# Splitting the key, value and query weights during the input projections, and starting the context attention inside the Fourier projection

## The chip, the cores and the metric

One core of one Trainium2 chip runs the whole program. The metric is the device time of that core in microseconds (us).

## What is computed

Two layers of a hybrid mixer over 512 latent tokens (stream X) and 256 context tokens (stream C), model width 1024, in float32. Cut to what matters here:

```python
for l in range(DEPTH):
    mod = silu_c @ w_mod[l] + b_mod[l]            # six rows: shift, scale, gate, twice
    h = x * (1 + sc1) + sh1
    proj = h @ w_in[l]                            # columns: A query/key-value/rope, B spatial gate, D pooling, C Fourier
    cq, ckv = rms_norm(proj[q]) , rms_norm(proj[kv])
    q = cq @ w_uq[l];  k = ckv @ w_uk[l];  v = ckv @ w_uv[l]
    attn = softmax(q k^T) v                       # 8 heads; context attends to context only
    mix = concat(attn, spatial_gating(proj), multiscale_pool(proj), fourier_mix(proj))
    x = layer_norm(ALPHA * x + g1 * (mix @ w_out[l]))
    x = layer_norm(ALPHA * x + g2 * swiglu(x * (1 + sc2) + sh2))
```

In layer 0 all four groups are computed for both streams, in layer 1 for X alone, with the context's keys and values.

## The kernel before

Every float32 product is made of three products of rounded halves. `split` (L167 to L169) turns a tile into a high part (a cast on ScalarE, L168) and a low part (a subtraction on VectorE, L169), and `mm3` (L172 to L174) issues low by high, high by low, high by high on TensorE.

A weight tile of the input projection is loaded by SyncE into a staging buffer (pool `S4`, four buffers, `wload`, L186) and split into a buffer of pool `W8` (five buffers). The projection's column groups have two weight tiles each, one per half of the 1024 rows: D0 and D4 for pooling, C0 and C4 for Fourier. `mods` (L268 to L308) computes later modulation rows from 512 KB tiles of `w_mod`, which go through the same `S4` buffers; L282 is their product, L301 and L308 their way into `modT`. Their steps are handed out by `fill` between the products of `chunk_d` and `chunk_c`, so that the loads of the next modulation run beside the projection.

After the A group, each layer calls `chunk_b` (gate columns, with a layer norm of 256 columns on VectorE and GpSimd, L375 to L541), `chunk_d` (pooling columns, four outputs in layer 0, two in layer 1, each of 24 products), `pool_sums` (running sums, L841 to L861), `spatial` (transposes at L811, products, gate at L822, transposes at L827), `pool_proj`, then `phase("att")`, which closes the scratch pool of the projections ("inp", ten buffers from `I`) and opens the attention's. Then come `make_ckv` (transposes at L602 and L606), `qkv_weights`, in layer 1 `make_cq` of X, and `chunk_c` (Fourier columns). `qkv_weights` loads `w_uk` and `w_uv` (L613, L614) into one `S4` tile and scales it (L615) and splits it, and loads the two halves of `w_uq` (L622), each into an `S4` tile, scales them (L625), splits them and copies rope columns on GpSimd (L632).

In layer 0 `chunk_c` runs to its end for both streams; then follow `make_cq(C)`, the Fourier transform and the context attention, which makes a head's query one step ahead of its scores (`make_q` for head h + 1 beside `scores` of head h).

The program is written in this order, but a scheduler that simulates the engines sets the final, fixed order of instructions on each engine, and with it which buffer of a pool each tile gets. Engines run their lists in that order. What it sets around the change is shown with the change, below.

Of the kernel before, what the change touches and what calls it, by code (L numbers as in the profile page):

```python
# [90 lines left out]
def hybrid_kernel(ctx: ExitStack, tc: tile.TileContext, out: bass.AP, g: dict):  # L91
# [453 lines left out]
    def chunk_c(l, streams):  # L545

        ws = [getw(("C", l, 0), 0), getw(("C", l, 4), 0)]
        for st in streams[::-1]:
# [16 lines left out]
            v = lambda ap: ap.rearrange("p n c -> p (n c)")  # L565
            split(v(st.f[0]), v(st.f[1]), pd[:, :n])

    def chunk_d(l, streams):
# [42 lines left out]
    def qkv_weights(l):  # L611
        st4 = S4(D)
        nc.sync.dma_start(out=st4[:, 0:512], in_=g["w_uk"][l])  # L613
# [6 lines left out]
        for k in range(2):  # L620
            st4 = S4(768)
            nc.sync.dma_start(out=st4, in_=g["w_uq"][l][k * P:(k + 1) * P, :])  # L622
            sc = ST(1)
            G_.tensor_scalar(out=sc, in0=pv(l, PQ, k), scalar1=QSCALE, scalar2=None, op0=ALU.mult)
            V_.tensor_scalar(out=st4, in0=st4, scalar1=sc, scalar2=None, op0=ALU.mult)  # L625
            w = W8()
            sv = st4.rearrange("p (h c) -> p h c", h=NH)
            wv = [w[:, i, :D].rearrange("p (h c) -> p h c", h=NH) for i in range(2)]
            split(wv[0][:, :, 0:96], wv[1][:, :, 0:96], sv)
            for i in range(2):  # L630
                for d_, s_ in ((96, 72), (104, 64), (112, 88), (120, 80)):
                    G_.tensor_copy(wv[i][:, :, d_:d_ + 8], wv[i][:, :, s_:s_ + 8])  # L632
            wq.append(wv)
# [118 lines left out]
    def attention(st, vt, wkv, wq):  # L752
# [30 lines left out]
        make_k(0, wkv, st)  # L783
        q[0] = make_q(st, 0, wq)
        for i, (h, qp) in enumerate(steps):
            if h % 2 == 0 and qp == 0:
                rv[h // 2] = rvp.tile([P, NTX, 2], F32, tag="rv", name=nm("rv"))
            es[(h, qp)] = scores(st, h, qp, q[h], rv[h // 2])
            if qp == 0 and h % 2 and h < NH - 1:
                make_k(h // 2 + 1, wkv, st)  # L790
            if qp == 0 and h < NH - 1:
                q[h + 1] = make_q(st, h + 1, wq)
            j = i - lagt
# [636 lines left out]
    for l in range(2):  # L1430
# [9 lines left out]
        if l == 1:  # L1440
            phase("inp")
        chunk_b(l, act)
        pts = chunk_d(l, act)
        dds = pool_sums(l, act, pts)
# [9 lines left out]
        if l == 1:  # L1454
            make_ckv(X, at)
        wkv, wq = qkv_weights(l)
        if l == 1:
            make_cq(X, at)
        chunk_c(l, act)
        fill(99)  # L1460
        if l == 0:
            make_cq(C, at)
        vt = []
        fo = fourier(l, act)
        if l == 0:
            values(wkv, vt, range(NTC))
            ac = attention(C, vt, wkv, wq)
            for i in range(NH):
# [57 lines left out]
```

## Time and profile before

| what | value |
|---|---|
| median of three runs | 1662.52 us (1662.23 to 1663.35) |
| profiled execution | 1662.84 us |
| its span | 1661.1 us |
| mean granted TensorE clock | 0.984 of full speed |
| TensorE busy | 1571.1 us, 95% |
| VectorE busy | 1048.2 us, 63% |
| ScalarE busy | 770.5 us, 46% |

The span is the stretch from the first to the last instruction that the profiler recorded; what lies around it is 1.7 us. The chain of work that ended last lies on TensorE for 80% of the span, on VectorE for 7%, on DMA for 5% and on ScalarE for 4%. The changed code runs at about 100 to 225 us (layer 0) and 1060 to 1120 us (layer 1).

### The profile page before, as it was taken

The numbers are of one execution on the slowest core, as the hardware profiler recorded it, in microseconds if no ns is written. First come the engines' busy times: TensorE is split into PE (matmuls) and PEld (weight loads), VectorE is DVE, ScalarE is ACT, GpSimd is POOL, SyncE is SP. The second block draws the span as 40 slices with busy tenths as digits, with TensorE's granted clock in tenths as the row PEclk, the third lists the DMA queues.
The fourth block names the chain that finished last, engine by engine and source line by source line (L and its number), as shares of the span: only waits on it lengthen the run. The fifth ranks groups of instructions, "written<-read, shape, count | busy, mean of one in ns | idle before, by whom it ended". The sixth has DMA issues, their size and how long they took to land.

```text
span 1661.1 us, 23839 instructions
## 1 busy us (share of the span) xinstructions
PE 1571.1 (95%) x9129; PEld 1357.4 (82%) x9129; DVE 1048.2 (63%) x1591; ACT 770.5 (46%) x1371; POOL 259.5 (16%) x322
## 2 busy tenths in 40 slices
PE   6999889999999999999999798989999999998897
PEld 3756778897899999997666486779988999997686
DVE  1433686876775656655435438577857888886835
ACT  2521675874643434434223525467954655554220
POOL 0213011430000000001205005243311000001302
PEclk9999999999999999999999898999999999999999
DMA  9566114118422323439886725411146344457321
GB/s 322 185 217 204 39 39 140 39 58 296 126 83 83 105 93 105 130 124 326 300 289 212 234 79 186 135 58 39 39 145 202 104 128 127 128 184 265 115 89 51
DMA packets 180502, 241.80 MB, mean 146 GB/s; under 512 B 10874, under 2 KB 127468, under 8 KB 180388
## 3 DMA queue, kind: packets, MB, share of 16 engines
q1 hardware_dynamic: 180388, 240.28, 44.7%
q8 instruction: 72, 1.18, 0.3%
q14 instruction: 42, 0.34, 0.1%
HBM read 215.30 MB, written 24.94 MB: 145 GB/s over the span
## 4 chain that ended last, share of the span: by engine, by line
PE 80%; DVE 7%; DMA 5%; ACT 4%; issue 2%; SPq 0%; POOL 0%; POOLq 0%; DVEq 0%; ACTq 0%
PE pd L1197 22%; PE pd L172 10%; PE pd L173 9%; PE pd L174 9%; PE ps L172 6%; PE ps L173 5%; PE ps L174 5%; PE ps L1197 4%; PE ps L282 3%; PE ps L739 3%; PE ps L723 2%; DVE w L169 2%; DVE u L169 2%; DMA s<-in_w_in_dram 2%; ACT w L168 1%
## 5 line engine op out<-in xcount | busy, mean ns | idle before, releaser
L169 DVE TENSOR_TENSOR w<-s,w 128x1024 fp32r<-128x1024 f32 (+3 forms) x285 | 353.9, 1248 | 276.5 <-ACT w L168 275.9
L168 ACT CAST w<-s 128x1024 fp32r<-128x1024 f32 (+3 forms) x285 | 292.8, 1030 | 464.7 <-PE pd L174 113.2
L1197 PE MATMUL pd<-u,w 128*128 128x256 f32 (+1 forms) x1938 | 298.3, 307 | 10.0 <-DVE w L169 8.7
L1197 PEld LDWEIGHTS pd<-u,w 128*128 128x128 f32 x1938 | 281.3, 190 | 16.6 <-DVE w L169 10.0
L172 PE MATMUL pd<-w,u 128*128 128x512 f32 (+5 forms) x728 | 276.8, 382 | 10.1 <-DVE u L169 3.1
L173 PE MATMUL pd<-w,u 128*128 128x512 f32 (+5 forms) x728 | 273.5, 376 | 1.7 <-DVE w L169 1.7
L174 PE MATMUL pd<-w,u 128*128 128x512 f32 (+5 forms) x728 | 271.0, 373 | 0.0
L172 PEld LDWEIGHTS pd<-w,u 128*128 128x128 f32 x728 | 139.4, 192 | 60.2 <-issue 19.3
L173 PEld LDWEIGHTS pd<-w,u 128*128 128x128 f32 x728 | 139.4, 192 | 29.1 <-issue 5.0
L174 PEld LDWEIGHTS pd<-w,u 128*128 128x128 f32 x728 | 139.3, 191 | 26.2 <-issue 3.4
L168 ACT CAST u<-y 128x512 fp32r<-128x512 f32 (+2 forms) x178 | 94.0, 546 | 76.8 <-DMA y<-yd 45.2
L169 DVE TENSOR_TENSOR u<-y,u 128x512 fp32r<-128x512 f32 (+2 forms) x118 | 79.4, 695 | 58.7 <-ACT u L168 52.6
L169 POOL TENSOR_TENSOR u<-y,u 128x512 fp32r<-128x512 f32 (+1 forms) x60 | 79.5, 1331 | 229.1 <-ACT u L168 207.5
L172 PE MATMUL ps<-u,w 128*128 128x256 f32 (+2 forms) x288 | 91.8, 327 | 1.8 <-DVE modT L308 1.2
L173 PE MATMUL ps<-u,w 128*128 128x256 f32 (+2 forms) x288 | 93.5, 327 | 0.1
L174 PE MATMUL ps<-u,w 128*128 128x256 f32 (+2 forms) x288 | 93.5, 327 | 0.0
L172 PE MATMUL ps<-w,u 128*128 128x512 f32 (+1 forms) x208 | 81.2, 399 | 6.1 <-DVE u L169 5.2
L173 PE MATMUL ps<-w,u 128*128 128x512 f32 (+1 forms) x208 | 82.2, 396 | 3.0 <-DVE w L169 3.0
L169 DVE TENSOR_TENSOR u<-ps,u 128x512 fp32r<-128x512 f32 (+2 forms) x106 | 66.9, 655 | 28.1 <-ACT u L168 27.0
L174 PE MATMUL ps<-w,u 128*128 128x512 f32 (+1 forms) x208 | 81.4, 392 | 0.0
L1313 POOL TENSOR_TENSOR f<-f,f 128x1024 f32<-128x1024 f32 x10 | 24.2, 2434 | 327.1 <-DMA f<-rd 248.5
L1197 PE MATMUL ps<-u,w 128*128 128x384 f32 (+1 forms) x456 | 73.8, 311 | 0.0
(250 smaller groups left out, 2588.8 us busy)
## 6 DMA issues: line engine op xcount, KB each, us to landing
s<-in_w_ffn_dram SPq DMA_DIRECT2D x154, 512.0 KB
s<-in_w_out_dram SPq DMA_DIRECT2D x50, 512.0 KB
u<-in_w_mod_dram SPq DMA_DIRECT2D x48, 512.0 KB
s<-in_w_mod_dram SPq DMA_DIRECT2D x48, 512.0 KB
s<-in_w_in_dram SPq DMA_DIRECT2D x16, 512.0 KB
yd<-f SPq DMA_DIRECT2D x19, 384.0 KB
y<-yd SPq DMA_DIRECT2D x88, 64.0 KB
y<-yd SPq DMA_DIRECT2D x22, 256.0 KB
```

Source lines behind the costliest of these rows:

```text
L168: A_.copy(out=hi, in_=src)
L169: (eng or V_).tensor_tensor(out=lo, in0=src, in1=f(hi), op=ALU.subtract)
L172: T_.matmul(ps, lhsT=ll, rhs=rh, start=start, stop=False)
L173: T_.matmul(ps, lhsT=lh, rhs=rl, start=False, stop=False)
L174: T_.matmul(ps, lhsT=lh, rhs=rh, start=False, stop=stop)
L282: T_.matmul(ps[32 * j:32 * j + 32, :n], lhsT=sst[:, k, :], rhs=ws[j // 2][:, (j % 2) * n:(j % 2 + 1) * n], start=(k == 0), stop=(k == KD - ...
L723: T_.transpose(pt[:, o:o + P], es[t2][:, k * P:(k + 1) * P], ident)
L739: T_.matmul(av[:, 0:256], lhsT=vt[k][:, h, :], rhs=pts[k // 2][:, a, (k % 2) * 256:(k % 2 + 1) * 256], start=(k == 0 and a == 1), stop=(k ...
L1197: T_.matmul(ps, lhsT=A[u][:, k], rhs=B[k][:, v], start=first and k == 0 and i == 0, stop=last and k == 3 and i == 2, skip_group_check=True)
L1313: G_.tensor_tensor(out=y, in0=y, in1=bc[0], op=ALU.mult)
```

## The change

`qkv_weights` is called right after `chunk_b`, ahead of `chunk_d`, and its staging tiles come from the scratch pool `I` in place of `S4`. `chunk_c` becomes a generator that stops after each stream, the context stream first. In layer 0, after that stop, `make_cq(C)` runs and the context attention starts: `make_k` for the first head pair and `make_q` for heads 0 and 1. Then `chunk_c` goes on with X. The context attention from there on makes its queries two heads ahead. No arithmetic is added or removed. In the listing of the changed kernel lines after L567 stand 1 later, after L785 6 later.

```diff
--- before.py
+++ after.py
@@ -564,6 +564,7 @@
                         w[0][:, k % 4], w[1][:, k % 4], k == 0, k == KD - 1)
             v = lambda ap: ap.rearrange("p n c -> p (n c)")
             split(v(st.f[0]), v(st.f[1]), pd[:, :n])
+            yield
 
     def chunk_d(l, streams):
 
@@ -609,7 +610,7 @@
             G_.tensor_copy(kT[i][64:P, :, sl], kT[0][64:P, :, sl])
 
     def qkv_weights(l):
-        st4 = S4(D)
+        st4 = I(n=D)
         nc.sync.dma_start(out=st4[:, 0:512], in_=g["w_uk"][l])
         nc.sync.dma_start(out=st4[:, 512:], in_=g["w_uv"][l])
         V_.tensor_scalar(out=st4, in0=st4, scalar1=pv(l, PKV, 0), scalar2=None, op0=ALU.mult)
@@ -618,7 +619,7 @@
 
         wq = []
         for k in range(2):
-            st4 = S4(768)
+            st4 = I(n=768)
             nc.sync.dma_start(out=st4, in_=g["w_uq"][l][k * P:(k + 1) * P, :])
             sc = ST(1)
             G_.tensor_scalar(out=sc, in0=pv(l, PQ, k), scalar1=QSCALE, scalar2=None, op0=ALU.mult)
@@ -782,14 +783,19 @@
 
         make_k(0, wkv, st)
         q[0] = make_q(st, 0, wq)
+        qa = 1
+        if st.s:
+            q[1] = make_q(st, 1, wq)
+            qa = 2
+            yield
         for i, (h, qp) in enumerate(steps):
             if h % 2 == 0 and qp == 0:
                 rv[h // 2] = rvp.tile([P, NTX, 2], F32, tag="rv", name=nm("rv"))
             es[(h, qp)] = scores(st, h, qp, q[h], rv[h // 2])
             if qp == 0 and h % 2 and h < NH - 1:
                 make_k(h // 2 + 1, wkv, st)
-            if qp == 0 and h < NH - 1:
-                q[h + 1] = make_q(st, h + 1, wq)
+            if qp == 0 and h < NH - qa:
+                q[h + qa] = make_q(st, h + qa, wq)
             j = i - lagt
             if j >= 0:
                 pts[steps[j]] = turn(st, es.pop(steps[j]))
@@ -1440,6 +1446,7 @@
         if l == 1:
             phase("inp")
         chunk_b(l, act)
+        wkv, wq = qkv_weights(l)
         pts = chunk_d(l, act)
         dds = pool_sums(l, act, pts)
         ahead(index[("C", l, 4)] + 1)
@@ -1453,18 +1460,20 @@
         make_ckv(C, at)
         if l == 1:
             make_ckv(X, at)
-        wkv, wq = qkv_weights(l)
+        vt = []
         if l == 1:
             make_cq(X, at)
-        chunk_c(l, act)
+        cc = chunk_c(l, act)
+        if l == 0:
+            next(cc)
+            make_cq(C, at)
+            ac = attention(C, vt, wkv, wq)
+            next(ac)
+        run(cc)
         fill(99)
-        if l == 0:
-            make_cq(C, at)
-        vt = []
         fo = fourier(l, act)
         if l == 0:
             values(wkv, vt, range(NTC))
-            ac = attention(C, vt, wkv, wq)
             for i in range(NH):
                 next(ac)
                 if i == XPREP:
```

The scheduler gives the instructions another order. In the order rows below `s`, `w` and `i` are buffers of `S4`, `W8` and `I`, the last number names the tile.

First place: SyncE in layer 0, from the loads of D4, C0 and C4 (L186) on. Before:

```order
L186 DMA s_159_1040<-in_w_in_dram 128x4x256
L186 DMA s_161_1045<-in_w_in_dram 128x4x256
L186 DMA s_163_1050<-in_w_in_dram 128x4x256
L268 DMA s_169_1074<-in_w_mod_dram 128x1024
L294 DMA gd<-y_1057 2x512 x2
L245 DMA y_1068<-in_b_mod_dram 2x512 x4
L268 DMA s_170_1076<-in_w_mod_dram 128x1024
L268 DMA s_172_1083<-in_w_mod_dram 128x1024
L268 DMA s_173_1085<-in_w_mod_dram 128x1024
L268 DMA s_175_1117<-in_w_mod_dram 128x1024
L874 DMA y_1367<-in_w_pool_dram 64x64 x4
```

And now:

```order
L186 DMA s_167_1079<-in_w_in_dram 128x4x256
L186 DMA s_169_1084<-in_w_in_dram 128x4x256
L186 DMA s_171_1089<-in_w_in_dram 128x4x256
L268 DMA s_177_1113<-in_w_mod_dram 128x1024
L294 DMA gd<-y_1096 2x512 x2
L245 DMA y_1107<-in_b_mod_dram 2x512 x4
L880 DMA y_1406<-in_w_pool_dram 64x64
L268 DMA s_178_1115<-in_w_mod_dram 128x1024
L880 DMA y_1406<-in_w_pool_dram 64x64 x3
L268 DMA s_180_1122<-in_w_mod_dram 128x1024
L614 DMA i_1040<-in_w_uk_dram 128x512
L615 DMA i_1040<-in_w_uv_dram 128x512
```

The four loads of `w_uk`, `w_uv` and `w_uq` (L614, L615, L623) now stand between the third and the fourth load of `w_mod` instead of behind all of them and `w_spatial`.

Second place: VectorE in layer 0. Tile 1040 before is D4, 1045 is C0, 1050 is C4. Before, from the split of D0 on:

```order
L169 TENSOR_TENSOR w_134_908<-s_133_907,w_134_908 128x1024
L169 TENSOR_TENSOR w_160_1041<-s_159_1040,w_160_1041 128x1024
L288 TENSOR_TENSOR y_1057<-ps_744,y_734 128x512
L169 TENSOR_TENSOR w_162_1046<-s_161_1045,w_162_1046 128x1024
L382 BN_STATS bn_971<-pd_730 128x6
L384 BN_AGGR st_973<-bn_971 128x2
L538 SCALAR_TENSOR_TENSOR i_968<-pd_730,st_973,y_964 128x256
L541 SCALAR_TENSOR_TENSOR i_968<-i_968,st_973,y_964 128x256
L169 TENSOR_TENSOR w_164_1051<-s_163_1050,w_164_1051 128x1024
```

Now D4 is tile 1079, and its split is the last of these rows, 39 rows behind D0's:

```order
L169 TENSOR_TENSOR i_1017<-i_1016,i_1017 128x256 x2
L616 TENSOR_SCALAR i_1040<-i_1040,PV 128x1024
L626 TENSOR_SCALAR i_1047<-i_1047,st_1049 128x768
L169 TENSOR_TENSOR w_160_1044<-i_1040,w_160_1044 128x1024
L626 TENSOR_SCALAR i_1063<-i_1063,st_1065 128x768
L169 TENSOR_TENSOR w_163_1052<-i_1047,w_163_1052 128x8x96
L169 TENSOR_TENSOR w_166_1068<-i_1063,w_166_1068 128x8x96
L169 TENSOR_TENSOR w_168_1080<-s_167_1079,w_168_1080 128x1024
```

The splits of D4, C0 and C4 left the place right behind D0's split; D4's now follows the scaling and splitting of the query, key and value weights, and C0's (tile 1085) and C4's (1090) come further behind, with pooling sums between.

TensorE in layer 0, where the first product with D4 stands (`w_168_1080` is D4 split, tiles 1122 and 1124 are loads of `w_mod`):

```order
L173 MATMUL ps_1216<-u_424,w_134_908 128x512
L174 MATMUL ps_1216<-u_424,w_134_908 128x512
L282 MATMUL ps_1117<-s_180_1122,sst 32x512 x2
L282 MATMUL ps_1117<-s_181_1124,sst 32x512 x2
L172 MATMUL ps_1130<-u_481,w_168_1080 128x512
L173 MATMUL ps_1130<-u_481,w_168_1080 128x512
```

Before, the 24 products of a pooling output (12 with D0, 12 with D4) stood in one row behind the first L282; now the twelve with D4 come after 36 with D0 and after four L282 rows, two of which follow each other. Of the 144 Fourier products (L172 to L174 with C0 and C4), 108 stood behind the transposes of `spatial` (L811) before; 52 stand behind them (L817) now, 56 went ahead of them.

Third place: TensorE in layer 1. Before, all 48 pooling products came first, then the transposes of `spatial` and the Fourier products:

```order
L173 MATMUL ps_9411<-u_8777,w_1479_9367 128x512
L174 MATMUL ps_9411<-u_8777,w_1479_9367 128x512
L811 MATMUL ps_9469<-ident,s_1496_9467 128x128 x4
L172 MATMUL pd_9631<-w_1481_9372,u_8721 128x256
L173 MATMUL pd_9631<-w_1481_9372,u_8721 128x256
L174 MATMUL pd_9631<-w_1481_9372,u_8721 128x256
```

Now the transposes (L817) come after 24 products with D0, and behind them one product with C0 (`w_1489_9411`) and then those with D4 (`w_1487_9406`):

```order
L174 MATMUL ps_9450<-u_8745,w_1464_9287 128x512
L817 MATMUL ps_9508<-ident,s_1504_9506 128x128 x4
L172 MATMUL pd_9631<-w_1489_9411,u_8721 128x256
L172 MATMUL ps_9516<-i_9320,u_9513 128x256
L172 MATMUL ps_9521<-i_9320,u_9513 128x256
L172 MATMUL ps_9422<-u_8753,w_1487_9406 128x512
L173 MATMUL ps_9422<-u_8753,w_1487_9406 128x512
```

VectorE in layer 1, ahead of these (9406 is D4, 9411 is C0 in their split forms; 9370, 9378 and 9394 are the key and value and the query weights):

```order
L626 TENSOR_SCALAR i_9373<-i_9373,st_9375 128x768
L538 SCALAR_TENSOR_TENSOR i_9319<-pd_9176,st_9357,y_9315 128x256
L626 TENSOR_SCALAR i_9389<-i_9389,st_9391 128x768
L169 TENSOR_TENSOR w_1479_9370<-i_9366,w_1479_9370 128x1024
L541 SCALAR_TENSOR_TENSOR i_9319<-i_9319,st_9357,y_9315 128x256
L169 TENSOR_TENSOR u_9513<-ps_9508,u_9513 128x512
L169 TENSOR_TENSOR w_1482_9378<-i_9373,w_1482_9378 128x8x96
L169 TENSOR_TENSOR w_1485_9394<-i_9389,w_1485_9394 128x8x96
L169 TENSOR_TENSOR w_1487_9406<-s_1486_9405,w_1487_9406 128x1024
L169 TENSOR_TENSOR w_1489_9411<-s_1488_9410,w_1489_9411 128x1024
```

D4 and C0 are split behind the three query, key and value splits; before, D4 was split ahead of the layer norm's rows (L382 to L541). On ScalarE the casts stand in the same succession, C0's as the last.

## Rows read from the trace of the kernel before

**Rows 1.** The profile page: span, TensorE's busy time, the chain by engine.

```profile
span 1661.1 us, 23839 instructions
...
PE 1571.1 (95%) x9129; PEld 1357.4 (82%) x9129; DVE 1048.2 (63%) x1591; ACT 770.5 (46%) x1371; POOL 259.5 (16%) x322
...
PE 80%; DVE 7%; DMA 5%; ACT 4%; issue 2%; SPq 0%; POOL 0%; POOLq 0%; DVEq 0%; ACTq 0%
```

**Rows 2.** Busy time by window, layer 0; columns: window, length, engines, PEclk, DMA, GB/s.

```profile
150.00:160.00 10.00, 10.00 (x75) 8.19 (x74) 5.82 (x6) 3.10 (x4) 5.72 (x7) 1.00 0.76 232
...
170.00:180.00 10.00, 6.72 (x42) 4.99 (x42) 8.82 (x23) 8.80 (x18) 0.00 (x0) 1.00 0.33 106
```

**Rows 3.** The same windows, layer 1.

```profile
1070.00:1080.00 10.00, 10.00 (x45) 8.09 (x44) 9.15 (x23) 4.89 (x10) 6.26 (x13) 1.00 0.32 94
```

**Rows 4.** Timeline of TensorE, layer 0: start us, us, instruction, idle before it.

```profile
112.74 1.05 PE L282 MATMUL ps<-s,sst 128*32 128x512 f32 x4
115.01 0.47 PE L172 MATMUL ps<-u,w 128*128 128x512 f32 x1 [1.22 <-DVE modT L308]
```

**Rows 5.** Chain of waits, layer 0, two loads of 512 KB: start us, us, what.

```profile
101.29 3.75 DMA s<-in_w_in_dram
...
107.44 3.90 DMA s<-in_w_in_dram
```

**Rows 6.** Timeline of TensorE, layer 1.

```profile
1069.85 0.39 PE L172 MATMUL ps<-u,w 128*128 128x512 f32 x1
...
1081.01 0.60 PE L811 MATMUL ps<-ident,s 128*128 128x128 f32 x4
...
1082.15 0.28 PE L172 MATMUL pd<-w,u 128*128 128x256 f32 x1
...
1084.51 0.28 PE L174 MATMUL pd<-w,u 128*128 128x256 f32 x1
...
1098.36 0.63 PE L606 MATMUL ps<-ident,u 128*128 128x128 f32 x4 [0.87 <-ACT y L884]
```

**Rows 7.** Timeline of SyncE's queue, layer 0.

```profile
148.73 0.33 SPq L613 DMA_DIRECT2D s<-in_w_uk_dram  x1
```

**Rows 8.** Timeline of VectorE, layer 0.

```profile
153.68 0.75 DVE L615 TENSOR_SCALAR s<-s,PV 128x1024 f32<-128x1024 f32 x1 [14.45 <-DMA s<-in_w_uv_dram]
```

**Rows 9.** Timeline of VectorE, layer 1.

```profile
1061.85 1.23 DVE L169 TENSOR_TENSOR w<-s,w 128x1024 fp32r<-128x1024 f32 x1
...
1075.60 0.42 DVE L382 BATCH_NORM_STATS2 bn<-pd 128x6 f32<-128x256 f32 x1
1075.94 0.41 DVE L169 TENSOR_TENSOR i<-i,i 128x256 fp32r<-128x256 f32 x1
...
1076.95 0.61 DVE L625 TENSOR_SCALAR s<-s,st 128x768 f32<-128x768 f32 x1
1077.48 0.48 DVE L538 SCALAR_TENSOR_TENSOR i<-pd,st,y 128x256 f32<-128x256 f32 x1
...
1080.34 0.94 DVE L169 TENSOR_TENSOR w<-s,w 128x768 fp32r<-128x768 f32 x1
...
1083.52 0.68 DVE L169 TENSOR_TENSOR u<-ps,u 128x512 fp32r<-128x512 f32 x1
```

**Rows 10.** Shorter windows of layer 0.

```profile
192.00:194.00 2.00, 0.97 (x9) 0.83 (x8) 1.17 (x4) 1.43 (x7) 0.00 (x0) 1.00 0.00 0
194.00:196.00 2.00, 1.41 (x11) 1.44 (x12) 1.85 (x4) 0.84 (x2) 0.00 (x0) 0.96 0.00 0
196.00:198.00 2.00, 2.00 (x12) 2.00 (x11) 0.97 (x3) 1.49 (x7) 0.00 (x0) 0.50 0.00 0
```

**Rows 11.** Timeline of ScalarE, layer 1.

```profile
1070.05 1.05 ACT L168 CAST w<-s 128x1024 fp32r<-128x1024 f32 x1 [2.21 <-PE pd L174]
...
1078.41 0.84 ACT L168 CAST w<-s 128x768 fp32r<-128x768 f32 x1
```

## The prediction, made before the run

> **What bounds the kernel now.** I read the page first: of a span of 1661.1 us TensorE is busy for 95%, and the chain that ended last lies on it for 80% [rows 1]. So a change that adds and removes no arithmetic is worth what it does to TensorE's idle time and to its granted clock. The windows of the two changed stretches come next, and they differ. While the query, key and value weights are scaled and split in layer 0, TensorE is busy for 10.00 of 10 us in the window from 150; it idles from 170 on, 3.28 of 10 us, in the attention's start [rows 2]. In layer 1 it is busy for 10.00 of 10 where pooling is projected [rows 3]. The splits that the change moves are therefore covered where they stand now; what they can be worth elsewhere is the idle time behind 170, and what they can cost lies where they go.
>
> The timelines and the chain then give durations. The L282 products on one `w_mod` load took 1.05 us [rows 4]. A 512 KB load took 3.75 and 3.90 us [rows 5]. A product of 512 columns takes a slot of 0.233 us: 48 of them lie between 1069.85 and 1081.01. One of 256 columns takes 0.118 us: 20 slots lie between 1082.15 and 1084.51 [rows 6].
>
> **Layer 0: the staging buffers.** The loads of D4, C0 and C4 are still issued right behind D0's, but their splits now stand behind the query, key and value splits, and the buffers bear it out: `W8` has five, handed out to D0, the three weights and D4 in this order, and C0 and C4 take D0's and D4's when these come free. So three of the four `S4` buffers hold unsplit tiles, and the loads of `w_mod` take turns in the one that is left: each is issued when the L282 of the load before it has ended, and lands 3.75 us later. I walk TensorE's new list from the point where both kernels agree, the first L282 of this modulation, which ends at 113.8 [rows 4].
> - Before, the next product waited 1.22 us for L308, which stood behind the last of the three splits on VectorE [rows 4]. That split is gone from there: -1.2.
> - Twelve products with D0 take 2.8 us, to 116.6. The second load was issued at 113.8 and lands at 117.5: +0.9. Its L282 ends at 118.5.
> - Twelve products of 256 and twelve of 512 columns take 1.4 and 2.8, to 122.7. The third load, issued at 118.5, is there. Its L282 ends at 123.7.
> - The next row is the L282 of the fourth load, issued at 123.7 at the earliest: it lands at 127.5. +3.8. It ends at 128.5.
> - The next product needs the low part of D4. The weights' four loads stand in SyncE's list behind the third `w_mod` load; before, 4.95 us passed from the issue of `w_uk` at 148.73 to the scaling at 153.68 [rows 7, 8]. Issued at 118.9, they let VectorE begin at 123.9. In front of D4's end lie one scaling of 0.75 [rows 8], two of 0.61, splits of 1.23, 0.94 and 0.94, and D4's own 1.23 [rows 9], 6.3 with what I round, so 130.3: +1.8.
>
> Sum for this stretch: +5.3. The bounds of the waits on loads: nothing, if the buffers come free earlier than the order says, and 8 us, if the loads lie beside the weights' 1.3 MB and take twice as long.
>
> **Layer 0: the attention's start.** Here the change does what it says: the context's queries and keys start in the middle of the Fourier products, and the next query stands two heads ahead. What could go is the idle time of 170 to 180, 3.28 us [rows 2], the idle 1.03 and 0.59 us between 192 and 196, and the stretch at a granted clock of 0.50 behind them, which from 194 to 202 costs 3.1 us [rows 10] (the row at 196 stands for three windows alike): 8.0 together. Against that, 56 of the 108 Fourier products that stood behind the transposes of `spatial` are ahead of them now. They are 56 x 0.118 = 6.6 us of work that covered the chains of `spatial` and pooling. I take 8.0 - 6.6 = 1.4 as the gain; the ends are 0 and 8.0. It is nearer the low end because each of these chains goes transposes, cast, subtraction, product, gate, and has no other work between.
>
> **Layer 1: the second place.** Before, D4 was split at 1061.85 [rows 9], ahead of the layer norm, and TensorE ran 48 pooling products without a pause [rows 6]. Now only 24 with D0 stand in front; they and the transposes are through at 1069.85 + 24 x 0.233 + 0.4 = 1075.9. The next row needs the high part of C0, which is the last cast of a row on ScalarE: the second weight tile's scaling, then casts of 0.84, 1.05 and 1.05 [rows 11]. VectorE reached the third tile's statistics at 1075.60 [rows 9], with the key and value split (1.23) already behind it. Without that split in front I set this at 1075.0. Up to the end of the last scaling follow 0.42, 0.41, 0.75, 0.61, 0.48, 0.61 and two short pieces, 0.6 together, so 1078.9 [rows 8, 9]; the casts end at 1081.8. TensorE waits 5.9 us. Then D4's low part: from 1078.9 VectorE has 1.23, 0.48, 0.68, 0.94, 0.94 and D4's 1.23 to do [rows 9], to 1084.4. Three products lie between, so the second wait is 1.8. Together +7.7, with bounds of 5 (ScalarE and VectorE close up the gaps between their rows) and 9. Fifteen Fourier products are left over behind this, and they cover the wait of 0.87 before the rope transposes at 1098.36 [rows 6]: -0.9. Net +6.8.
>
> **The clock.** Pauses of 1.03 and 0.59 us were followed by a granted clock of 0.50 [rows 10], the lower of the two levels, 1.2 GHz; but 3.28 idle us in ten left it at 1.00 [rows 2]. The new pauses, 3.8 and 1.8 us with one us of work between, and 5.9 and 1.8 with three products between, are longer than either. I take one fall in each layer at the 3.1 us of that row: +6.2. A slower TensorE gives the other engines the same time to catch up, and the short waits behind both places, about one us in each layer, go under it: -2.0. Without both falls this term is 0, with a third one +7.3. The Trainium skill, in "TensorE: Matmul & The Clock Gate", section "HAM oscillation — how this bites in real kernels", says that a wait for data that is long enough halves the clock of the products behind it, and advises to put the products of one tile together before one waits for the next; this speaks against the new order, in which D0's and D4's products are taken apart. By that rule both falls come, and the sum stands as it is; by the 170 window alone it would be 4.2 less.
>
> **Costed at nothing:** the rope copies and the two scalings of `sc` on GpSimd, which are moved ahead of its pooling sums and are through before TensorE hands over the pooling columns that these sum; the two more query buffers, since `U` has 22; the reordering behind the common point in both layers, where the lists agree again.
>
> **The sum.** 5.3 - 1.4 + 6.8 + 6.2 - 2.0 = +14.9 on the profiled execution's 1662.84 us: 1677.7. The median of the runs is 0.3 lower, so 1677.4.
>
> **Rivals.**
> 1. The waits come, the clock stays. For it: the window at 170 [rows 2]. Against it: the pauses are three times as long as those that were followed by a fall. +10.7: 1673.2. With one fall, 1675.3. Chance 0.3 together.
> 2. Faster: the change does what it says, and no wait takes the place. Then -1.2 at 115, the whole 8.0 behind 170 at best, -0.9 in layer 1; with half of the 8.0, -6: 1656.5. The point that decides is whether D4's split in layer 0 is done when its first product comes up, which asks that the weights land by 118 and not 124; the 4.95 us from issue to use [rows 7, 8] speak against it. The Trainium skill, "DMA: Bandwidth & Descriptors", section "Rules for kernel authors", speaks for it: issue a transfer early, compute, wait late. By that rule moving the weights' loads ahead by 30 us is a gain. The trace shows VectorE idle for 14.45 us before the scaling [rows 8] while TensorE is busy for 10.00 of 10 [rows 2], so the time so gained is not TensorE's. Chance 0.11.
> 3. Even: the reordered attention gives back its 8.0, the clock holds, and layer 1's wait is at its low end. 4.1 + 5 - 8 = about +1, so 1663.5. Chance 0.05 for within 0.2%, and as much for a little above it.
> 4. Worse: loads that take twice as long beside each other, and a third fall, +6 more: 1683. Chance 0.09.
>
> **The numbers.** My forecast has 0.4. 0.2%, 3.3 us, is about what a measurement of this kernel can tell from no change. The range from 1662 to 1684 takes in the forecast, rivals 1, 3 and 4, and leaves out 2 and what lies beyond. Faster 0.11, same 0.05, slower 0.84.
>
> **What would show it.** In layer 0, around 123 to 131, two waits of TensorE, one on a `w_mod` load before an L282, one on VectorE before the first product with D4; loads of `w_mod` one after the other through one buffer; the granted clock at 0.5 for some us behind. In layer 1, a wait of about 6 us on ScalarE's cast behind the transposes of `spatial`, then a shorter one on D4's subtraction, where the window from 1070 had none. Around 170 to 200, fewer idle us than before. Wrong would be: pooling's products without a pause in either layer, D4 split ahead of the query weights, or a total that comes from another stretch.

## The result, and the profile after

The changed kernel is slower by about 1%: 1680.9 us (median of 4, 1680.06 to 1681.76) against 1662.93 us (median of 4), a ratio of 1.0103 with a 95% interval of 1.0088 to 1.0119. The forecast was 1677.4 us, the range 1662 to 1684. Measured again later (e10), beside 20 runs of the kernel before, the ratio was 1.0116 (1.0094 to 1.0138).

The page of the profiled execution (1680.06 us); it answers to [rows 1]:

```profile
span 1678.3 us, 23832 instructions
...
PE 1577.6 (94%) x9129; PEld 1360.9 (81%) x9129; DVE 1044.9 (62%) x1591; ACT 770.1 (46%) x1371; POOL 265.0 (16%) x322
...
PE 80%; DVE 9%; DMA 5%; ACT 4%; issue 2%; POOL 0%; SPq 0%; DVEq 0%; POOLq 0%; ACTq 0%
```

TensorE's busy time grew by 6.5 us although it issues the same 9129 products, and the span by 17.2. What is added is idle time and products at the lower clock, in places that the windows name. First four of layer 0, then one of layer 1; they answer to [rows 2, 3] (the columns are those of [rows 2]):

```profile
120.00:130.00 10.00, 5.96 (x32) 3.73 (x28) 5.25 (x11) 4.02 (x9) 2.41 (x5) 0.99 0.71 236
130.00:140.00 10.00, 8.69 (x31) 4.82 (x33) 3.12 (x4) 2.37 (x3) 5.06 (x15) 0.67 0.37 112
...
170.00:180.00 10.00, 9.20 (x78) 8.82 (x76) 4.78 (x8) 3.63 (x5) 0.00 (x0) 1.00 0.24 71
180.00:190.00 10.00, 6.84 (x40) 5.08 (x40) 7.62 (x22) 6.68 (x17) 0.00 (x0) 1.00 0.30 101
...
1080.00:1090.00 10.00, 4.45 (x15) 3.30 (x14) 9.22 (x14) 5.46 (x8) 9.19 (x20) 0.77 0.33 79
```

In layer 0 the window from 120 has only 5.96 busy us of 10, and the one from 130 a granted clock of 0.67. In layer 1, which now begins about 5 us later, the window from 1080 has 4.45 of 10 where [rows 3] had 10.00 from 1070. TensorE's timeline names the waits (in brackets the idle time and what ended it): five of layer 0, three of layer 1, one at the end of the program.

```profile
114.38 1.05 PE L282 MATMUL ps<-s,sst 128*32 128x512 f32 x4 [0.75 <-DMA s<-in_w_mod_dram]
...
119.47 1.05 PE L282 MATMUL ps<-s,sst 128*32 128x512 f32 x4 [1.07 <-DMA s<-in_w_mod_dram]
121.06 0.39 PE L172 MATMUL ps<-u,w 128*128 128x256 f32 x1 [0.53 <-ACT i L540]
...
130.12 1.92 PE L282 MATMUL ps<-s,sst 128*32 128x512 f32 x4 [3.63 <-DMA s<-in_w_mod_dram]
133.23 0.79 PE L172 MATMUL ps<-u,w 128*128 128x512 f32 x1 [1.19 <-DVE w L169]
...
1086.00 0.58 PE L172 MATMUL pd<-w,u 128*128 128x256 f32 x1 [4.92 <-ACT w L168]
...
1087.73 0.80 PE L172 MATMUL ps<-u,w 128*128 128x512 f32 x1 [0.63 <-DVE w L169]
...
1116.12 0.75 PE L172 MATMUL ps<-w,ckvT 128*128 128x512 f32 x1 [2.91 <-DVE kT L169]
...
1570.87 0.80 PE L173 MATMUL ps<-w,u 128*128 128x512 f32 x1 [6.94 <-DVE w L169]
```

Shorter windows show what follows the pauses: the clock falls to 0.50, the 1.2 GHz level, four times in the changed stretches. It does so behind 130, behind 1086 and behind 1116, and from 191 to 194 behind five short waits of the attention's start (0.87, 0.36, 0.21, 0.42 and 0.57 us between 185 and 190.2).

```profile
128.00:130.00 2.00, 0.00 (x0) 0.00 (x0) 2.00 (x4) 0.83 (x1) 0.72 (x2) 0.94 0.60 224
130.00:132.00 2.00, 1.88 (x4) 0.19 (x4) 1.95 (x4) 1.78 (x2) 2.00 (x4) 0.50 0.00 0
132.00:134.00 2.00, 0.81 (x4) 0.67 (x3) 1.18 (x1) 0.00 (x0) 2.00 (x7) 0.50 0.44 76
134.00:136.00 2.00, 2.00 (x7) 1.52 (x6) 0.00 (x0) 0.00 (x0) 1.06 (x6) 0.50 0.94 369
136.00:138.00 2.00, 2.00 (x9) 1.28 (x9) 0.00 (x0) 0.11 (x1) 0.00 (x0) 0.86 0.24 88
...
190.00:192.00 2.00, 1.87 (x10) 1.70 (x11) 1.69 (x5) 0.26 (x1) 1.17 (x2) 0.80 0.00 0
192.00:194.00 2.00, 2.00 (x8) 1.71 (x7) 1.27 (x3) 1.78 (x5) 0.00 (x0) 0.50 0.00 0
...
1084.00:1086.00 2.00, 0.00 (x1) 0.01 (x1) 2.00 (x4) 2.00 (x4) 2.00 (x6) 0.87 0.18 67
1086.00:1088.00 2.00, 1.37 (x4) 1.05 (x5) 2.00 (x3) 0.25 (x1) 2.00 (x3) 0.50 0.00 0
...
1116.00:1118.00 2.00, 1.88 (x5) 1.49 (x6) 1.97 (x4) 1.06 (x3) 1.87 (x2) 0.55 0.73 199
1118.00:1120.00 2.00, 2.00 (x7) 1.59 (x6) 2.00 (x4) 0.94 (x2) 0.16 (x1) 0.60 0.35 141
```

A place that both kernels pass tells how much was lost by then. Taken from the two timelines of TensorE:

| place | before | after | difference | gained or lost there | forecast |
|---|---|---|---|---|---|
| bias transposes (L231), unchanged code | 65.84 | 66.86 | +1.0 | +1.0 | 0 |
| transposes of `spatial`, layer 0 (less 6.6 us of products moved ahead of them) | 153.80 | 169.66 | +9.3 | +8.3 | 5.3 + 3.1 |
| nine softmax transposes of the context attention (L723, L724) | 246.42 | 252.55 | +6.1 | -3.2 | -1.4 - 1.0 |
| last transposes of layer 1's projection (L368), same order | 1040.11 | 1045.22 | +5.1 | -1.0 | 0 |
| last softmax transposes, layer 1 | 1220.80 | 1235.48 | +14.7 | +9.6 | 6.8 + 3.1 - 1.0 |
| end of the span | 1661.1 | 1678.3 | +17.2 | +2.5 | 0 |

The two forecast places carry 8.3 and 9.6 us. In the first row and the fourth the lists of TensorE are the same in both kernels; that they cancel out is chance. The last row was not forecast.

Three more views show the mechanism. SyncE's queue in layer 0: the second, third and fourth load of `w_mod` are issued at 115.47, 120.56 and 126.54, each just after the L282 of the load before it, and each of the three L282 in the fence of waits above waits for its load (the third load's L282, at 125.44, does not). Before, four went out one right behind the other, from 111.83 on.

```profile
109.28 0.46 SPq L268 DMA_DIRECT2D s<-in_w_mod_dram  x1
...
115.47 0.34 SPq L268 DMA_DIRECT2D s<-in_w_mod_dram  x1
...
120.56 0.33 SPq L268 DMA_DIRECT2D s<-in_w_mod_dram  x1
120.94 0.43 SPq L614 DMA_DIRECT2D i<-in_w_uk_dram  x1
...
126.54 34.50 SPq L268 DMA_DIRECT2D s<-in_w_mod_dram  x13
```

VectorE in layer 0: the scaling of the key and value weights starts at 125.87, when they land, and D4's split comes last, at 131.92; the first D4 product is at 133.23.

```profile
125.87 0.75 DVE L616 TENSOR_SCALAR i<-i,PV 128x1024 f32<-128x1024 f32 x1 [3.15 <-DMA i<-in_w_uv_dram]
...
131.92 1.25 DVE L169 TENSOR_TENSOR w<-s,w 128x1024 fp32r<-128x1024 f32 x1
```

VectorE in layer 1, from the third tile's statistics (L382) on: scalings, the key and value split, and D4's and C0's splits last, as one row at 1086.42. TensorE began to wait at 1081.1 (the window from 1080 in steps of 2 us has 1.08 busy, the next none).

```profile
1079.22 0.42 DVE L382 BATCH_NORM_STATS2 bn<-pd 128x6 f32<-128x256 f32 x1
...
1081.99 0.60 DVE L626 TENSOR_SCALAR i<-i,st 128x768 f32<-128x768 f32 x1
1082.52 1.21 DVE L169 TENSOR_TENSOR w<-i,w 128x1024 fp32r<-128x1024 f32 x1
...
1086.42 2.42 DVE L169 TENSOR_TENSOR w<-s,w 128x1024 fp32r<-128x1024 f32 x2
```

### The profile page after: what moved, and what is told of

The parts are those of the page before. It is cut to its first block, busy times and chain, and to the rows that moved or that the text cites. A ratio compares the mean times of both kernels' runs of the same rounds, so it can differ in the third digit from the quotient of the medians.

```text
span 1678.3 us, 23832 instructions
## 1 busy us (share of the span) xinstructions
PE 1577.6 (94%) x9129; PEld 1360.9 (81%) x9129; DVE 1044.9 (62%) x1591; ACT 770.1 (46%) x1371; POOL 265.0 (16%) x322
## 4 chain that ended last, share of the span: by engine, by line
PE 80%; DVE 9%; DMA 5%; ACT 4%; issue 2%; POOL 0%; SPq 0%; DVEq 0%; POOLq 0%; ACTq 0%
PE pd L1203 21%; PE pd L172 10%; PE pd L173 10%; PE pd L174 9%; PE ps L172 6%; PE ps L173 5%; PE ps L174 5%; PE ps L1203 4%; PE ps L282 3%; PE ps L740 3%; DVE w L169 2%; PE ps L724 2%; DVE u L169 2%; DMA u<-in_w_mod_dram 1%; ACT w L168 1%
## 5 line engine op out<-in xcount | busy, mean ns | idle before, releaser
L169 DVE TENSOR_TENSOR w<-s,w 128x1024 fp32r<-128x1024 f32 (+2 forms) x279 | 346.0, 1246 | 266.8 <-ACT w L168 266.2
L168 ACT CAST w<-s 128x1024 fp32r<-128x1024 f32 (+2 forms) x279 | 287.2, 1033 | 444.5 <-PE pd L1203 117.4
L172 PE MATMUL pd<-w,u 128*128 128x512 f32 (+5 forms) x728 | 276.3, 381 | 10.2 <-ACT w L168 6.8
L174 PE MATMUL pd<-w,u 128*128 128x512 f32 (+5 forms) x728 | 270.6, 373 | 0.0
L172 PEld LDWEIGHTS pd<-w,u 128*128 128x128 f32 x728 | 138.7, 191 | 61.6 <-issue 21.0
L174 PEld LDWEIGHTS pd<-w,u 128*128 128x128 f32 x728 | 138.7, 190 | 26.4 <-issue 3.4
L172 PE MATMUL ps<-u,w 128*128 128x256 f32 (+2 forms) x288 | 94.1, 335 | 3.5 <-DVE w L169 1.8
L173 PE MATMUL ps<-u,w 128*128 128x256 f32 (+2 forms) x288 | 94.8, 331 | 0.1
L174 PE MATMUL ps<-u,w 128*128 128x256 f32 (+2 forms) x288 | 94.4, 330 | 0.0
L172 PE MATMUL ps<-w,u 128*128 128x512 f32 (+1 forms) x208 | 81.4, 400 | 6.5 <-DVE u L169 5.3
L174 PE MATMUL ps<-w,u 128*128 128x512 f32 (+1 forms) x208 | 82.0, 395 | 0.0
```

Of the source, the lines that this page charges most:

```text
L168: A_.copy(out=hi, in_=src)
L169: (eng or V_).tensor_tensor(out=lo, in0=src, in1=f(hi), op=ALU.subtract)
L172: T_.matmul(ps, lhsT=ll, rhs=rh, start=start, stop=False)
L173: T_.matmul(ps, lhsT=lh, rhs=rl, start=False, stop=False)
L174: T_.matmul(ps, lhsT=lh, rhs=rh, start=False, stop=stop)
```

## The experiments

Theory A: the loss comes from the splits of D4, C0 and C4, which now stand behind the query, key and value splits; the attention's new order gains. Rival B: the loss comes from the 56 Fourier products that no longer cover `spatial` and pooling. Rival C: the part of the loss at the end of the program (the tail, in the last feed-forward) comes from any reordering. Ratios are to the kernel before on the same chip, with 95% intervals. Edits are shown against the changed kernel, in e2 against the kernel before; `...` stands for lines left out.

### e1: the attention's part alone

```diff
         chunk_b(l, act)
-        wkv, wq = qkv_weights(l)
         pts = chunk_d(l, act)
...
+        wkv, wq = qkv_weights(l)      # behind make_ckv, staged in S4
         vt = []
```

> Only the second half of the change: chunk_c by stream, the context attention started in its middle, queries two ahead; the query, key and value weights are loaded, staged and split where they were before. Theory A (the loss comes from the splits of D4, C0 and C4 standing behind the query, key and value splits): no loss, 1657 to 1663 us, no wait of TensorE over 1 us on a w_mod load around 110 to 135 and none on ScalarE's cast around 1080. Rival B (the loss comes from the Fourier products that no longer cover spatial and pooling): 1668 us or more, with the waits behind 160. Rival C (the tail's part, 2.6 us, comes from any reordering ahead): about 2.6 us of it appear at the end in either case.

Measured: 1658.84 us, ratio 0.9968 (0.9953 to 0.9982): a gain of 5.3 us. Between 100 and 150 TensorE waits once, 1.15 us for L308 as before, and layer 1's waits are those of the kernel before. Three windows of layer 0:

```profile
170.00:180.00 10.00, 7.09 (x48) 5.61 (x47) 8.47 (x22) 8.32 (x18) 0.00 (x0) 1.00 0.33 107
180.00:190.00 10.00, 9.43 (x70) 8.93 (x71) 7.19 (x16) 6.26 (x14) 1.17 (x2) 1.00 0.01 2
190.00:200.00 10.00, 10.00 (x89) 10.00 (x89) 7.20 (x15) 7.28 (x20) 2.16 (x3) 1.00 0.17 53
```

From 180 on TensorE is nearly filled and the clock stays at 1.00; the fall of [rows 10] does not come. So with these weights in the old place the attention's new order costs nothing. Rival B is not tested here: 36 of the 144 Fourier products stand ahead of the transposes of `spatial`, as before, so none is moved. e3 and e7 test it, and the section on the prediction gives its size.

### e2: the moved weights alone

```diff
         chunk_b(l, act)
+        wkv, wq = qkv_weights(l)      # staged in I
         pts = chunk_d(l, act)
```

> Only the first half: the query, key and value weights right behind chunk_b, staged in the projection's scratch; chunk_c and the attention as before. Theory A: nearly the whole loss, 1675 to 1683 us, with the two waits in layer 0 (about 3.6 us on a w_mod load, about 1.2 us on D4's subtraction), the wait of about 5 us on C0's cast in layer 1, and a granted clock of 0.5 behind each. Rival B: 1660 to 1666 us.

Measured: 1678.23 us, ratio 1.0079 (1.0056 to 1.0102). Layer 0 has the waits (6.3 us on `w_mod` loads, 1.8 on D4's subtraction). Layer 1's wait on C0's cast is there, but only 1.83 us long, and the clock behind it stays at 1.00, so this part of the expectation was wrong. (A wait of 2.94 us on a split of `kT` at 1121.71 is followed by 0.50 here too, as in the changed kernel.) VectorE's list tells why the first wait is short:

```profile
1083.15 0.75 DVE L615 TENSOR_SCALAR i<-i,PV 128x1024 f32<-128x1024 f32 x1 [1.24 <-DMA i<-in_w_uv_dram]
1085.07 1.22 DVE L169 TENSOR_TENSOR w<-i,w 128x1024 fp32r<-128x1024 f32 x1 [1.16 <-ACT w L168]
1087.21 0.43 DVE L382 BATCH_NORM_STATS2 bn<-pd 128x6 f32<-128x256 f32 x1 [0.92 <-PE pd L174]
```

Here the scheduler put the scaling and the split of the key and value weights ahead of the layer norm's statistics (L382, 1087.21), in time that VectorE had free; in the changed kernel they stand behind the third tile's. The same source lines of layer 1 thus got another order. That different simulated times ahead of them are the reason is likely, but not shown.

### e3 and e4: the full change, with D4, C0 and C4 first

e3 adds one line, e4 moves the call behind `chunk_d`:

```diff
         chunk_b(l, act)
+        ahead(index[("C", l, 4)] + 1)        # e3
         wkv, wq = qkv_weights(l)
         pts = chunk_d(l, act)
```

```diff
         chunk_b(l, act)
-        wkv, wq = qkv_weights(l)
         pts = chunk_d(l, act)
+        wkv, wq = qkv_weights(l)             # e4
```

> The full change with one line more: the projection's remaining weight tiles (D4, C0, C4) are handed their buffers ahead of the query, key and value weights, so that they are split right behind D0's as before. Theory A: the waits of layer 0 and layer 1 go, 1656 to 1664 us. Rival B: the waits behind 160 stay, 1668 us or more. If it is the early loads of the weights themselves that disturb w_mod's loads, the waits on w_mod loads in layer 0 stay, 1666 us or more.

> The full change with the call of qkv_weights one line further down, behind chunk_d. Theory A: as the run before, 1656 to 1664 us, since D4, C0 and C4 are split first here too. Rival B: 1668 us or more.

Measured: 1659.23 us, ratio 0.9968 (0.9954 to 0.9983), and 1659.54 us, 0.9965 (0.9952 to 0.9979). The first two rows of the waits of e3's layer 1 between 1050 and 1140, the longest there (columns: total, times, longest):

```profile
PE pd L172 <- POOL u L169: 1.4, 1, 1.4
PE pd L172 <- ACT e L694: 1.0, 1, 1.0
```

Neither C0's cast nor D4's subtraction is among them, and in layer 0 no wait on a `w_mod` load exceeds 0.4 us. So theory A holds: the early loads, the staging in the scratch and 33 of the 56 Fourier products ahead of `spatial` remain in e3, and the loss is gone with the order of the splits. For the rest of rival B there is e7 (below), which has 66 more products ahead of the transposes than the kernel before and still runs at 1.0011. e3 also shows what the moved weights are worth when they harm nothing: e3 loads `w_uk` at 123.91, e1 at 149.92, and they are equally fast. The rule on early transfers that the prediction weighed (the Trainium skill, "DMA: Bandwidth & Descriptors", section "Rules for kernel authors") finds no gain here, as [rows 2] had it.

### e5 and e6: the moved call in one layer

`qkv_weights` takes the pool of its staging tiles as a second argument here; where it is called in the old place that is `S4`.

```diff
...
-        wkv, wq = qkv_weights(l)
+        if l == 0:                           # e6: l == 1
+            wkv, wq = qkv_weights(l)
         pts = chunk_d(l, act)
...
+        if l == 1:                           # e6: l == 0
+            wkv, wq = qkv_weights(l, S4)
```

> The full change, but in layer 1 the query, key and value weights are loaded, staged and split where they were before; only layer 0 has the moved call. Theory A, which puts 7 us of loss on the moved weights in layer 1 with its falls of the clock: 1666 to 1672 us; layer 0 with its wait of about 3.6 us on a w_mod load, layer 1 without the wait on C0's cast. If the attention's gain already pays for layer 0's waits: 1662 to 1666.

> The full change, but in layer 0 the query, key and value weights are loaded, staged and split where they were before; only layer 1 has the moved call. Theory A: 1664 to 1670 us, the attention's gain of 5 less layer 1's loss; the wait of about 5 us on C0's cast behind the transposes of spatial, no waits on w_mod loads in layer 0. If layer 1's wait is covered as in the run of the first half alone (1.8 us, no fall of the clock): 1658 to 1663.

Measured: 1671.26 us, ratio 1.0052 (1.0033 to 1.0071), and 1668.52 us, 1.0036 (1.0020 to 1.0051). Against e1's 0.9968 the moved call costs 0.84% or 14 us in layer 0 and 0.68% or 11 us in layer 1; with e1's gain of 5 that makes 20, of which the changed kernel shows 17 to 19. The waits sit where theory A puts them: 3.7 us on a `w_mod` load and 1.2 on D4 in e5, 4.95 on C0's cast in e6. The attention's gain does not pay for layer 0. (In e5 and e6 the tail has the other order too. Against e1 it is longer by 0.2 us in e5's trace and by 2.0 in e6's, from the last softmax transposes to the end, so up to 2 of e6's 11 us may belong there.)

### e7: only D4 first

```diff
         chunk_b(l, act)
+        ahead(index[("D", l, 4)] + 1)
         wkv, wq = qkv_weights(l)
```

> The full change, but of the three tiles only D4 is handed its buffer ahead of the query, key and value weights; C0 and C4 stay behind them, so that two of the four staging buffers are held instead of three. If the wait on D4's split does the harm: both waits of layer 0 small, layer 1 with 48 pooling products in a row and a wait of about 3 us on C0's cast, 1660 to 1668 us. If the held staging buffers do it: waits on w_mod loads of 2 us or more stay in layer 0.

Measured: 1665.64 us, ratio 1.0011 (1.0001 to 1.0020). One row of the waits of layer 0, one of layer 1:

```profile
PE ps L282 <- DMA s<-in_w_mod_dram: 1.6, 3, 1.2
...
PE pd L173 <- DVE w L169: 2.3, 1, 2.3
```

With two staging buffers held in place of three, the waits on `w_mod` loads fall from 5.4 us (their sum in the changed kernel's waits of layer 0) to 1.6. In layer 1 the pooling products run through, and C0 is waited for behind them, 2.3 us, for its subtraction, one instruction later than expected. Both tiles thus take part in layer 1, D4 and then C0. In layer 0 the loss is gone: the stretch from L231 to the transposes of `spatial` takes 87.2 us, less the 66 moved products, against 88.0 before. There D4's early split and the freed third buffer came in one edit; their waits are separate rows, but their prices are not taken apart. Against e3's 0.9968, C0 and C4 behind the weights cost 0.4%, 7 us; of these the traces show 4.0 in layer 1 and 2.9 in the tail, which has the other order in e7.

### e8 and e9: early start and second query apart

Both have the weights in the old place. The edit of e8 to the attention:

```diff
         q[0] = make_q(st, 0, wq)
         qa = 1
         if st.s:
-            q[1] = make_q(st, 1, wq)         # e8: early start, one ahead
-            qa = 2
             yield
```

e9 is the kernel before with `qa = 2` for the context and no early start.

> The second half of the change (weights in the old place) without its queries two ahead: chunk_c by stream and the context attention started in its middle, the next query one head ahead. If the early start makes the gain: 1657 to 1661 us as with both. If the second query ahead makes it: 1662 to 1666 us, the waits behind 186 as in the kernel before.

> The kernel before with one thing of the change: the context attention makes its queries two heads ahead; it starts where it did, and the weights stay where they were. If the early start inside chunk_c alone makes the attention's gain: no difference from the kernel before, 1661 to 1667 us. If the second query ahead makes a gain of its own when the attention starts late: 1657 to 1660 us.

Measured: e8 1659.20 us, ratio 0.9974 (0.9963 to 0.9985); e9 1661.24 us, 0.9981 (0.9968 to 0.9994). Each alone gains 3 to 4 us, both together 5. The expectation that only one of them counts was wrong. In the traces they share a part: the wait of 1.00 us at 189.67 in the kernel before goes in both; the one of 1.62 us behind it [rows 10] goes in e8, while e9 has one of 1.75 there, without a fall of the clock. That 3 and 4 make 5 and not 7 lies within the intervals as well.

### e10: the changed kernel again, and e11: an early start in layer 1

> The changed kernel once more, on the chip and beside the runs of the kernel before that the parts were compared with. If the parts add up (attention -5, layer 0 +12 to 13, layer 1 +10): +17 us, 1680 to 1684. The tail, 2.6 us longer in the first profile: again a wait of about 7 us on VectorE in the last feed-forward with a lower clock behind it, if that comes from the order there; shorter, if it was that one execution.

Measured: 1682.88 us, ratio 1.0116 (1.0094 to 1.0138). The tail is there again; VectorE and TensorE in it:

```profile
1558.69 11.22 DVE L169 TENSOR_TENSOR u<-y,u 128x512 fp32r<-128x512 f32 x4
...
1572.24 0.80 PE L173 MATMUL ps<-w,u 128*128 128x512 f32 x1 [6.59 <-DVE w L169]
```

e11 is e3 with layer 1's attention begun ahead of its Fourier products:

```diff
-            yield
+        yield
...
             next(ac)
+        else:
+            ax = attention(X, vt, wkv, wq)
+            next(ax)
         run(cc)
...
             ax = attention(X, vt, wkv, wq)
+            next(ax)
...
```

The stop at the start of the attention now holds for X too, in layer 0 as well, where one more `next(ax)` answers it.

> The third run's kernel (D4, C0, C4 first) with the attention of layer 1 also begun ahead of its Fourier products. If the waits of layer 1's attention (4 us between 1098 and 1116 in the kernel before) can be covered like layer 0's: 1654 to 1657 us. If the scheduler leaves the transposes of the rope and of the keys behind the Fourier products, nothing changes: 1657 to 1661.

Measured: 1660.71 us, ratio 0.9986 (0.9971 to 1.0001): no better than e3. The scheduler left the rope and key transposes behind the Fourier products, and the waits behind them stay: 4.7 us in four waits from 1091 to 1109, in e3 4.8 in five. The total does not tell of layer 1 alone, because TensorE's list of layer 0 changed too (from 222 to 345 us) and the tail has the other order.

## Why the prediction was right

**Layer 0, staging buffers.** Right in mechanism and size. The walk had waits of 0.9, 3.8 and 1.8 us and 1.2 gained; the trace has 1.07, 3.63 and 1.19 of these, and two that the walk had not: 0.75 on the first load and 0.53 on a copy by ScalarE (L540). About 0.4 of the 0.75 is not the order's: e3 and e6, whose splits stand in layer 0 as before, wait 0.39 and 0.41 there. With 1.22 gained that is +5.95 against +5.3. e3 and e5 show that the waits hang on the order of the splits.

**Layer 0, attention's start.** The net of the stretch was forecast at -1.4 (with 1.0 more hidden under the slower clock), measured at -3.2. The sign was right; both sizes were too large, and that their difference came near is luck. The step was built as 8.0 that could go less 6.6 of cover that was lost. In e1, where no Fourier product is moved, the stretch from the transposes of `spatial` to the nine softmax transposes takes 86.6 us (155.00 to 241.60) in place of 92.6: 6.0 could go, not 8.0. In the changed kernel it takes 82.9, and with the 6.6 us of the moved products 89.5 (e5 and e10: 89.2 and 89.6). So the 56 products cost 2.9 us and not 6.6. TensorE's waits in this stretch sum to 12.7 us before, 9.6 in e1 and 10.1 in the changed kernel: little cover was lost. Of the 2.9, 1.7 is the clock, which falls from 191 to 194 in the changed kernel and not in e1; e6, where no product is moved, has such a fall too (0.50 from 182 to 184), so that it comes from the moved products is not shown. This is also what rival B of the experiments is worth: at most 3 of the 17 us. Of the 14 us that the moved call costs in layer 0 by the ratios, the traces of e5 and e1 show 11.8: 9.2 ahead of the transposes of `spatial` and 2.6 behind; the rest lies within the intervals.

**Layer 1.** The two waits came in the places named, 4.92 and 0.63 us against 5.9 and 1.8. The wait began at 1081.1, which is the 1075.9 of the forecast and the 5.1 us by which layer 1 began later. e6 shows it at 4.95 us with layer 0 undisturbed, and e2 at 1.83 with another order on VectorE. Both waits were too large in the forecast, 7.7 us together against 5.6. The term that failed is the -0.9 behind: left-over Fourier products were to cover the wait before the rope transposes. They did, and the next wait grew: 2.91 us for a split of `kT` on VectorE, 0.80 before (at 1102.03 in TensorE's timeline), and with it a third fall of the clock. That split came at 1115.38, behind two splits of the Fourier tables' tiles at 1112.28 and 1114.12; before, these were over by 1098.3, ahead of it. The errors cancel, which is luck: the sum was 8.9 against 9.6.

**The clock.** Two falls were forecast at 3.1 us each. They came, three windows at 0.50 each (130 to 136, and 1086 to 1092). Half of the busy time in them is 2.3 and 2.7 us, and 0.3 and 0.2 come from the window behind: 2.6 and 2.9, less than forecast because TensorE waited in part of that time. The third, in layer 1, cost 1.7 (0.55 and 0.60), and the one from 191 cost 1.7 (0.80, 0.50 and 0.85), where the forecast had no fall left. Rival 1, in which the clock stays, did not come. The reason that the forecast gave was misread, though. The idle 1.03 and 0.59 us of [rows 10] are one wait of 1.62, which the border of the windows cuts at 194, and the kernel before has a longer one 15 us ahead of it, behind which the clock stayed at 1.00 in the windows from 178 to 184:

```profile
179.50 0.39 PE L172 MATMUL pd<-w,u 128*128 128x258 f32 x1 [1.77 <-DVE u L169]
...
194.59 0.36 PE L172 MATMUL ps<-kT,u 96*128 96x256 f32 x1 [1.62 <-DVE u L169]
```

So the new pauses of 3.8 and 5.9 us were 2.3 and 3.6 times as long as that wait, not "three times as long" as two, and the length of a wait did not decide alone. The conclusion held: the waits of 3.63 to 4.21 us on a `w_mod` load in the changed kernel, e2, e5 and e10, and those of 4.92 to 4.95 on C0's cast in the changed kernel, e6 and e10, were all followed by a fall.

**Costed at nothing.** This step failed in one place. It said that the lists agree again behind the common point, but in the last feed-forward they do not, and the span ends 2.5 us later than that point gives. In the traces the whole change is 17.2 us against 14.9 forecast; this is about the difference. VectorE splits four activation tiles there (`u<-y`, 128x512). Before, in the timelines of VectorE, GpSimd and TensorE, with GpSimd's sums (L1314) beside it up to 1552:

```profile
1546.92 6.91 DVE L169 TENSOR_TENSOR u<-y,u 128x512 fp32r<-128x512 f32 x4
...
1545.88 6.19 POOL L1314 TENSOR_TENSOR f<-f,f 128x1024 f32<-128x1024 f32 x2
...
1556.16 0.50 PE L173 MATMUL ps<-w,u 128*128 128x512 f32 x1 [3.00 <-DVE w L169]
```

After, in the timelines of VectorE and GpSimd, where the scheduler put one GpSimd sum more beside them:

```profile
1557.32 11.22 DVE L169 TENSOR_TENSOR u<-y,u 128x512 fp32r<-128x512 f32 x4
1568.47 1.21 DVE L189 TENSOR_TENSOR s<-s,f 128x1024 f32<-128x1024 f32 x1
...
1559.63 8.37 POOL L1320 TENSOR_TENSOR f<-f,f 128x1024 f32<-128x1024 f32 x3
```

The four took 11.22 us instead of 6.91, and TensorE waited 6.94 instead of 3.00 for the weight split behind them, with the clock at 0.50 after. e10 shows the same 11.22 and 6.59. But other waits of the tail went in exchange (4.61 us at 1506.05 and 2.43 at 1541.50 before, 2.80 at 1519.23 after). From the last softmax transposes of layer 1 to the end TensorE's waits sum to 16.8 us before and 17.2 after, while half of its busy time at 0.50 is 3.4 and 6.4: the 2.5 us are the clock behind the long wait. Rival C of the experiments, that any reordering ahead changes the tail, is not borne out: e3 and e8 keep the order of before there, and e1, e4 and e9 all but a few rows of VectorE. Over the experiments the stretch from the first product of the last feed-forward to the end of the span was 347 to 350 us where the tail had the order of before, and 350 to 351 with the other order. Of the kernels with the old order, the kernel before, e3 and e8 take 347, without a fall behind this wait, and e1, e4 and e9 take 349 to 350, with one. So the changed kernel's 350 is no more than the old order with a fall takes. What the new order costs by itself is not shown; no kernel was run to take this apart.

**The rivals.** The gain (rival 2) needed D4's split to be done in time; e3 and e4 make it so and gain 5 us. So rival 2's mechanism was right for a kernel one line away, and the point from which it decides, when D4 is split, was the right one. Its size, 6 us, was near too. But e1 gains as much with the weights in their old place, so the gain is the attention's alone. Rival 4 had a third fall and loads that take twice as long; the fall came, the slow loads did not.

## What to carry to other kernels

When a step that takes buffers of a rotating pool is moved ahead of others that take theirs from the same pool, look which tiles now wait for a buffer or stand behind it in an engine's list, and which staging buffers they hold meanwhile. Here one line that hands the older tiles their buffers first turned 17 us of loss into 5 of gain. Moving work out of a stretch where TensorE is already filled gained nothing here (e3 against e1). A pause that two windows share looks like two short ones; read its length from the timeline. And lists far behind a change are to be compared too when a scheduler makes them.

## What the runs showed of the hardware that was not expected

The same wait does not always lower the clock. TensorE's wait on VectorE in the tail took 3.00, 2.96, 2.94 and 2.95 us in the kernel before, e3, e1 and e4; the granted clock behind it was 1.00, 1.00, 0.57 and 0.50. All longer waits there were followed by 0.50: 3.03 us (e9), 3.26 (e6), 4.71 (e7), 6.10 (e11), 6.59 (e10), 6.94 (the changed kernel) and 7.18 (e5). Shorter waits went either way as well. In the attention's start of layer 0 a wait of 1.77 or 1.78 us left the clock at 1.00 in the kernel before, e1 and e9 and was followed by 0.50 in e6 and e8, and in the kernel before so was the one of 1.62 us [rows 10]. So profiles of kernels that wait alike can differ by a fall, and each of the four falls in the changed kernel's stretches cost 1.7 to 2.9 us. Whether executions of one kernel differ in this way is hardly shown: only the changed kernel was profiled twice, with the same four falls. Differences of that size need many runs.

VectorE's split of an activation tile (`u<-y`, 128x512) took 0.69 us where GpSimd was idle (at 1093.80 in the kernel before) and 2.8 to 2.9 us each, 11.22 for four, beside GpSimd's sums in the changed kernel's tail. In the kernel before the first two of the four took 2.9 each and the last two, begun after these sums had ended at 1552.07, 0.68. The Trainium skill, "GPSIMD Engine Reference", section "Specifications", says that GpSimd shares its memory interfaces with VectorE and that instructions with two inputs in that memory contend; the trace agrees, with four times the duration.
